# Seven block products for the gates of branches two and three and the recurrence's inputs, in a hybrid diffusion step

## The chip, the cores and the metric

The kernel runs on one core of one Trainium2 chip. The metric is the device time of one execution in microseconds, the median of several runs. A core has TensorE (PE, matrix products into PSUM), VectorE (DVE), ScalarE (ACT) and GpSimd (POOL); SyncE (SP) issues the transfers. Each engine runs its own instructions in a fixed order and waits for the others by semaphores.

## The reference, cut to what matters

One step of a two-layer backbone on 128 context tokens and 512 latent tokens, all float32, width 1024. Each layer:

```python
h = rms_norm(x, norm1_g) * (1 + scale1) + shift1
z = h @ w_in
u_pool, q, k, v, u_lru, u_gate, gates = jnp.split(z, splits, axis=-1)
pool_o = pool_mixer(u_pool, w_pool, pool_scale)                 # branch one
attn_o = neighbourhood_attention(...)                           # branch two (context tokens: full attention)
h_seq, h_final = rg_lru(conv_centred(u_lru, conv_w, conv_b), ...)   # a linear recurrence both ways
lru_o = h_seq * jax.nn.gelu(u_gate)                             # branch three
g = jax.nn.sigmoid(gates.reshape(B, L, 3, D_MODEL))
merged = (g[:, :, 0] * (pool_o @ w_branch[0]) + g[:, :, 1] * (attn_o @ w_branch[1])
          + g[:, :, 2] * (lru_o @ w_branch[2]))
x = x + gate1 * (merged @ w_out)
h2 = rms_norm(x, norm2_g) * (1 + scale2) + shift2
x = x + gate2 * (jnp.square(jax.nn.relu(h2 @ w_up)) @ w_down)
```

`shift1` to `gate2` come from a product of the conditioning vector with `w_mod` (1024 x 6144). `w_in` has 6144 columns: 512 each for u_pool, q, k, v, u_lru and u_gate, then 3 x 1024 for the gates.

## The kernel before

All 640 tokens stand on the free axis, in two halves of 320; channels stand on the partitions. A float32 product is made of three matmuls in a reduced format: each operand is split into a high and a low part, and high x high, high x low and low x high are added up in PSUM. Weights are split when they arrive (ScalarE copies the high part, L227, VectorE subtracts for the low part, L228), activations when they are made.

The work is a list of items. An item is one block of weights with the code that uses it: `k8` is 1024 rows x 128 columns (8 blocks of 128 rows, `product`, L256 to L258), `k4` is 512 rows x 256 columns, `modv` is a block of `w_mod` that VectorE alone multiplies and adds up (`mod_acc`, L517 and L519), and `st` is a pair, 1024 rows x 256 columns, as seven block products. The loop at the end goes through the items: transfers are issued up to three items ahead into three raw tiles of 512 KB (a pair takes two), weights are split one item ahead, then the item's body runs. `mod_next` puts the next `modv` item into the list.

A pair (`st_begin`, `st_product`, `st_body`) is a Winograd form of Strassen's scheme: the weights are seen as 2 x 2 blocks (512 rows x 128 columns), the activations as 2 x 2 blocks (512 channels x 320 tokens). POOL makes four sums of weight blocks (S1 to S4, L272 to L275), the seven blocks a11, S1, S2, a12, S3, S4, a22 are split one after another (L288, L289), each is multiplied with one of the seven activation blocks b11, T1, T2, b21, T3, b22, T4 (12 matmuls each, L295 to L297), and the results are added up: in PSUM where the order allows, else copied out by ScalarE (`keep`, L309) and added by VectorE (`total`, L313). T1 to T4 are made by `sums` from the four blocks of h. Before, only the MLP's first matrix is used in this way, from block 1 on; `sums` runs at the head of the MLP.

Side work stands in Python generators in two queues, `side_a` (attention, norms) and `side_b` (pool mixing, the recurrence `lru`, `sums`). `tick()` after each product runs one step of each, `drain` runs a queue to its end, `defer` puts a piece behind so many ticks. The framework orders the instructions of an engine by this order of tracing and by when their operands are ready in its own model.

A layer, in order: 16 items of w_in for v, k, q and the pool with attention as side work; the gates of branch one (8 `k8` items) with its branch products (4 `k4`); the recurrence's inputs (4 items) and the GELU inputs (4 items) in the order `ORD`; the gates and products of branch two; those of branch three; the output projection; the MLP. The recurrence `lru` runs as side work from its first item to the start of branch three's products. The MLP's head is four `k8` items at once (`head`): their low halves, then the norm of the second half of the tokens (`norm_second`), the rest of the first half with its evictions (L1190 to L1193), and the second half. Then two plain items, two `down` items and the first pair.

Large tiles come from one pool `act` of 13 tiles of 10 KB a partition: x, h, v, q/k, branch operands, T1 to T4. The attention's masks `um` and its probabilities `P` have tiles of their own. `xs_d` is a copy of x in device memory; x is read back for the output projection.

## Time and profile before

| | us |
|---|---|
| median of 3 runs | 2134.58 (2133.09 to 2137.39) |
| the profiled execution | 2134.76 |
| its span, first to last instruction | 2133.0 |
| TensorE busy | 2095.2 (98%) |
| VectorE busy | 1487.4 (70%) |
| ScalarE busy | 1009.3 (47%) |
| POOL busy | 524.5 (25%) |

In the first layer the span runs so: branch one from 216 to 329 us (with the attention's end), the recurrence's and GELU's inputs from 329 to some 400, the products of branch two from 412 on, those of branch three from 504.7, the output projection from 579.6, the MLP head from 640 to 705.6, the rest of the MLP to some 1085. The second layer follows in the same order, its MLP head from 1685 to 1752.2, and ends at 2133. A busy share counts an instruction from its start to its end; matmuls overlap, so the share of TensorE says only that it hardly pauses. Weight loads (PEld) run beside the matmuls.

### The profile page before, as it was taken

The numbers are of one execution on the slowest core, as the hardware profiler recorded it, in microseconds if no ns is written. First come the engines' busy times: TensorE is split into PE (matmuls) and PEld (weight loads), VectorE is DVE, ScalarE is ACT, GpSimd is POOL, SyncE is SP. The second block draws the span as 40 slices with busy tenths as digits, with TensorE's granted clock in tenths as the row PEclk, the third lists the DMA queues.
The fourth block names the chain that finished last, engine by engine and source line by source line (L and its number), as shares of the span: only waits on it lengthen the run. The fifth ranks groups of instructions, "written<-read, shape, count | busy, mean of one in ns | idle before, by whom it ended". The sixth has DMA issues, their size and how long they took to land.

```text
span 2133.0 us, 35830 instructions
## 1 busy us (share of the span) xinstructions
PE 2095.2 (98%) x13916; PEld 1985.1 (93%) x13916; DVE 1487.4 (70%) x2925; ACT 1009.3 (47%) x2058; POOL 524.5 (25%) x567
## 2 busy tenths in 40 slices
PE   8999999999999999999999999999999999999999
PEld 3988899999999999999989888999999999999999
DVE  4776865757669877777687685575667786666665
ACT  4765526664345433333366653367623543333332
POOL 2444300333203221111134440013311231121110
PEclk9999999999999999999999999999999999999999
DMA  9322244325541433333331122442345212222222
GB/s 322 109 60 85 64 135 120 87 88 158 158 115 52 120 102 98 99 99 99 119 117 52 55 74 79 144 119 65 90 124 186 76 50 80 81 83 84 81 80 79
DMA packets 248961, 218.16 MB, mean 102 GB/s; under 512 B 11076, under 2 KB 216408, under 8 KB 248792
## 3 DMA queue, kind: packets, MB, share of 16 engines
q1 hardware_dynamic: 248792, 215.88, 33.5%
q8 instruction: 109, 1.79, 0.4%
q14 instruction: 60, 0.49, 0.1%
HBM read 204.76 MB, written 13.12 MB: 102 GB/s over the span
## 4 chain that ended last, share of the span: by engine, by line
PE 80%; DVE 10%; ACT 4%; DMA 3%; issue 1%; POOL 1%; SPq 0%; ACTq 0%; DVEq 0%; POOLq 0%
PE mm L256 19%; PE mm L257 18%; PE mm L258 18%; PE mm L295 4%; PE mm L297 4%; PE mm L296 4%; PE o L772 2%; DVE wlo L228 2%; PE mmz L296 1%; PE mmz L297 1%; PE mmz L295 1%; DVE t L465 1%; DVE macc L519 1%; PE ptt L759 1%; PE mps L1438 1%
## 5 line engine op out<-in xcount | busy, mean ns | idle before, releaser
L256 PE MATMUL mm<-h,whi 128*128 128x320 f32 x1600 | 507.3, 317 | 10.3 <-DVE rl L1190 7.2
L258 PE MATMUL mm<-h,wlo 128*128 128x320 f32 x1600 | 498.1, 311 | 3.1 <-DVE wlo L228 3.0
L257 PE MATMUL mm<-h,whi 128*128 128x320 f32 x1600 | 498.3, 311 | 2.7 <-DVE h L479 2.0
L228 DVE TENSOR_TENSOR wlo<-raw,whi 128x512 fp32r<-128x512 f32 x396 | 287.4, 735 | 112.6 <-ACT whi L227 110.7
L227 ACT ACTIVATE whi<-raw 128x512 fp32r<-128x512 f32 x396 | 243.5, 626 | 231.4 <-PE mm L257 86.3
L256 PEld LDWEIGHTS mm<-h,whi 128*128 128x128 f32 x1600 | 303.5, 190 | 25.6 <-ACT h L478 7.6
L256 PE MATMUL mm<-u,whi 128*128 128x320 f32 x992 | 308.2, 311 | 4.1 <-DVE x L498 3.4
L257 PEld LDWEIGHTS mm<-h,whi 128*128 128x128 f32 x1600 | 303.6, 190 | 5.4 <-DVE h L479 2.9
L258 PEld LDWEIGHTS mm<-h,wlo 128*128 128x128 f32 x1600 | 303.4, 190 | 4.2 <-DVE wlo L228 4.1
L258 PE MATMUL mm<-u,wlo 128*128 128x320 f32 x992 | 306.5, 309 | 0.0
L257 PE MATMUL mm<-u,whi 128*128 128x320 f32 x992 | 306.5, 309 | 0.0
L498 DVE SCALAR_TENSOR_TENSOR x<-mm,mod,x 128x320 f32<-128x320 f32 (+2 forms) x432 | 175.3, 433 | 116.7 <-PE mm L258 116.3
L519 DVE SCALAR_TENSOR_TENSOR macc<-raw,silc,macc 128x512 f32<-128x512 f32 x280 | 217.5, 799 | 36.8 <-DMA raw<-in_w_mod_dram 35.1
L256 PEld LDWEIGHTS mm<-u,whi 128*128 128x128 f32 x992 | 186.2, 188 | 8.6 <-issue 3.9
L257 PEld LDWEIGHTS mm<-u,whi 128*128 128x128 f32 x992 | 186.3, 188 | 0.1
L258 PEld LDWEIGHTS mm<-u,wlo 128*128 128x128 f32 x992 | 186.2, 188 | 0.0
L272 POOL TENSOR_TENSOR S<-raw 128x512 f32<-128x512 f32 x26 | 34.3, 1320 | 531.8 <-DMA raw<-in_w_up_dram 319.6
L288 ACT ACTIVATE whi<-S 128x512 fp32r<-128x512 f32 x104 | 65.8, 633 | 198.6 <-PE mm L257 144.0
L288 ACT ACTIVATE whi<-raw 128x512 fp32r<-128x512 f32 x78 | 49.4, 633 | 127.1 <-PE mm L257 106.6
L289 DVE TENSOR_TENSOR wlo<-S,whi 128x512 fp32r<-128x512 f32 x104 | 73.0, 703 | 44.4 <-ACT whi L288 44.1
L297 PE MATMUL mm<-T,wlo 128*128 128x320 f32 x312 | 96.5, 309 | 0.5 <-DVE wlo L289 0.5
L295 PE MATMUL mm<-T,whi 128*128 128x320 f32 x312 | 96.4, 309 | 0.0
(303 smaller groups left out, 4657.6 us busy)
## 6 DMA issues: line engine op xcount, KB each, us to landing
raw<-in_w_in_dram SPq DMA_DIRECT2D x96, 512.0 KB, 4.1
raw<-in_w_mod_dram SPq DMA_DIRECT2D x80, 512.0 KB, 3.8
raw<-in_w_up_dram SPq DMA_DIRECT2D x64, 512.0 KB, 3.8
raw<-in_w_down_dram SPq DMA_DIRECT2D x64, 512.0 KB, 3.5
raw<-in_w_branch_dram SPq DMA_DIRECT2D x24, 512.0 KB, 3.5
wm<-in_w_mod_dram SPq DMA_DIRECT2D x8, 1024.0 KB, 12.2
raw<-in_w_out_dram SPq DMA_DIRECT2D x16, 512.0 KB, 4.6
xs_d<-x SPq DMA_DIRECT2D x4, 1280.0 KB, 7.8
```

The lines of the kernel that those rows point to most:

```text
L227: A.activation(hi, rs, AF.Copy)
L228: V.tensor_tensor(lo, rs, f32(hi), op=OP.subtract)
L256: T.matmul(ps, wh, xh, start=(k == 0), stop=False)
L257: T.matmul(ps, wh, xl, start=False, stop=False)
L258: T.matmul(ps, wl, xh, start=False, stop=(k == nk - 1))
L288: A.activation(hi, a, AF.Copy)
L289: V.tensor_tensor(lo, a, f32(hi), op=OP.subtract)
L295: T.matmul(ps, hi[:, k, :], x[:, 0, k, :], start=start and k == 0, stop=False, skip_group_check=True)
L296: T.matmul(ps, hi[:, k, :], x[:, 1, k, :], start=False, stop=False, skip_group_check=True)
L297: T.matmul(ps, lo[:, k, :], x[:, 0, k, :], start=False, stop=k == 3, skip_group_check=True)
L498: V.scalar_tensor_tensor(xa, ps[:, a:b], mod[l][:, gate + m, j:j + 1], xa, op0=OP.mult, op1=OP.add)
L519: V.scalar_tensor_tensor(acc[j], w, silc[:, k, j:j + 1], acc[j], op0=OP.mult, op1=OP.add)
```

## The change

Four pairs per layer take the place of the eight plain items for the recurrence and GELU inputs, and eight pairs that of the sixteen gate items of branches two and three (`z_pair`). For this `sums` now also runs in branch one, from gate 4 on, and again at the MLP head for the new h. A pair needs less room: S1, S2 and S4 follow one another in one tile, S3 overwrites a21, and each sum is made when the split before it has read its place. The tile Z of a pair comes from the PSUM pool that the attention's output has. `tick` inside a pair steps the side queues after every other product only.

`um` and `P` move into one tile `room` of the pool `act`, which gets 14 tiles; it is given back at gate 4, where the attention is driven to its end. The order of inputs is now recurrence 0 and 1, GELU 0 and 1, GELU 2 and 3, recurrence 2 and 3. Modulation items: 4 stand among the inputs where 6 stood, 8 in branch three where 12 stood; four move to the plain items and first `down` items of the MLP, and three further places are added there.

The norm of the second half becomes four pieces of two channel blocks, one at once and one after each of the next three evictions; `sums` is queued after them. The first output product does the first six blocks of both halves, then the last two.

The diff, without the moved code, comments, the changed lines of the loops that call it, and the removed functions that the new ones replace:

```diff
-    act = pool("act", 13)
+    act = pool("act", 14)
...
-    s_p = pool("s", 3)
...
-    um = [cst.tile([128, n], F32, name=f"um{i}") for i, n in enumerate((640, 384, 384))]
...
-        s1, s2, s3, s4 = (t_p.tile([128, 4, 128], F32, tag="t", name=f"S{i}") for i in range(1, 5))
-        G.tensor_tensor(s1, a21, a22, op=OP.add)
-        G.tensor_tensor(s2, s1, a11, op=OP.subtract)
-        G.tensor_tensor(s3, a11, a21, op=OP.subtract)
-        G.tensor_tensor(s4, a12, s2, op=OP.subtract)
-        it["todo"] = deque([a11, s1, s2, a12, s3, s4, a22])
+        s = t_p.tile([128, 4, 128], F32, tag="t", name="S")
+        sub = lambda o, a, b: lambda: G.tensor_tensor(o, a, b, op=OP.subtract)
+        G.tensor_tensor(s, a21, a22, op=OP.add)
+        G.tensor_tensor(a21, a11, a21, op=OP.subtract)
+        it["todo"] = deque([(a11, None), (s, sub(s, s, a11)), (s, sub(s, a12, s)), (a12, None), (a21, None), (s, None),
+                            (a22, None)])
...
-        a = it["todo"].popleft()
+        a, then = it["todo"].popleft()
...
+        if then:
+            then()
...
-        Z = s_ps.tile([128, HALF], F32, tag="s", name="mmz")
+        Z = o_ps.tile([128, HALF], F32, tag="o", name="mmz")
...
-                ahead()
-            tick()
+                nx = it["i"] + 2
+                while nx < len(items) and items[nx - 1]["kind"] == "modv":
+                    nx += 1
+                splits(nx)
...
-    def head(its, done, evict, second=None):
+    def head(its, done, evict, second=None, third=None):
...
+        drain(side_a)
+        if third:
+            third()
...
-        norm_stats(1)
-        norm_apply(l, which, 1)
+
+        def steps():
+            norm_stats(1)
+            for m in range(0, 8, 2):
+                norm_apply(l, which, 1, m, m + 2)
+                yield
+        side_a.append(("norm", steps()))
+        step(side_a)
...
-                P = s_p.tile([128, 384], F32, tag="s", name="P")
+                P = L["P"][0]
+                L["P"].rotate(-1)
...
+    def z_pair(l, L, ci, handlers, pre=None, last=False):
+        def body(it):
+            if "T" not in L:
+                drain(side_b)
+            st_body(it, L["T"], lambda m, half, t: handlers[m](half, t))
+            if last:
+                del L["T"]
+        add("st", w_in[l][:, ci * 128:ci * 128 + 256], body, pre)
...
+                drain(side_a)
...
+            room = unit("room", [128, 2560], F32)
+            L["um"] = [room[:, a:b] for a, b in ((0, 640), (640, 1024), (1024, 1408))]
+            L["P"] = deque(room[:, 1408 + 384 * i:1792 + 384 * i] for i in range(3))
+            for t, a in zip(L["um"], (256, 192, 64)):
+                G.memset(t[:, a:a + 128], 0.0)
...
-        def pre_b(b):
-            def fn():
-                flush()
-                if b == 0:
-                    drain(side_b, ("pool", 3))
-                    L["bo", 0] = L["pool"]
-                    L["merged"] = [unit(f"mg{i}", [128, 4, 640], F32) for i in range(2)]
-                elif b == 1:
-                    drain(side_a)
-                    L["bo", 1] = split_act(L, L.pop("attn"), "ah")
-                    L.pop("v")
-                else:
-                    drain(side_b)
-                    L["bo", 2] = split_act(L, L.pop("lru"), "lh")
-                    L["mh"] = [[unit(f"mh{a}{b}", [128, 2, 4, HALF]) for b in range(2)] for a in range(2)]
-            return fn
-
-        for b in range(3):
-            if b == 1:
-                need_lru = lambda: L.__setitem__("lru", unit("lru", [128, 4, 640], F32))
-                for n, i in enumerate(ORD):
-                    if 0 < n < 7:
-                        mod_next()
-                    if i < 4:
-                        z_item(l, L, COL_GELU + i, gelu_handler(l, L, i))
-                    else:
-                        z_item(l, L, COL_LRU + i - 4, lru_handler(l, L, i - 4), need_lru if i == 4 else None)
-            for m in range(0, 8, 2):
-                for e in range(3):
-                    if e < 2:
-                        z_item(l, L, COL_GATE + 8 * b + m + e, gate_handler(L, b, m + e))
-                    else:
-                        branch_item(l, L, b, m, pre_b(b) if m == 0 else None)
-                    if b != 1:
-                        mod_next()
...
-            while "h free" not in L:
+            while ("free", which) not in L:
...
+        def pre_branch(b, m):
+            def fn():
+                flush()
+                if (b, m) == (0, 0):
+                    drain(side_b, ("pool", 3))
+                    L["bo", 0] = L.pop("pool")
+                    L["merged"] = [unit(f"mg{i}", [128, 4, 640], F32) for i in range(2)]
+                elif (b, m) == (2, 0):
+                    L.pop(("bo", 1))
+                    drain(side_b)
+                    L["bo", 2] = split_act(L, L.pop("lru"), "lh")
+                    L["mh"] = [[unit(f"mh{a}0", [128, 2, 4, HALF])] for a in range(2)]
+                else:
+                    L["merged"][0] = None
+                    for a in range(2):
+                        L["mh"][a].append(unit(f"mh{a}1", [128, 2, 4, HALF]))
+            return fn if (b, m) in ((0, 0), (2, 0), (2, 4)) else None
+
+        def pre_sums():
+            drain(side_a)
+            for k in ("v", "um", "P"):
+                L.pop(k)
+            side_b.append(("sums", sums(0)))
+
+        def pre_lru():
+            flush()
+            L.pop(("bo", 0))
+            L["bo", 1] = split_act(L, L.pop("attn"), "ah")
+            L["lru"] = unit("lru", [128, 4, 640], F32)
+
+        def last_gate(it):
+            L["free", 0] = True
+
+        for b in range(3):
+            if b == 1:
+                for n, (col, fn) in enumerate(((COL_LRU, lru_handler), (COL_GELU, gelu_handler), (COL_GELU + 2, gelu_handler),
+                                               (COL_LRU + 2, lru_handler))):
+                    ct = 2 * (n > 1)
+                    z_pair(l, L, col, [fn(l, L, ct + e) for e in range(2)], pre_lru if n == 0 else None)
+                    mod_next()
+            for m in range(0, 8, 2):
+                if b == 0:
+                    for e in range(2):
+                        z_item(l, L, COL_GATE + m + e, gate_handler(L, b, m + e), pre_sums if m + e == 4 else None,
+                               last_gate if m + e == 7 else None)
+                        mod_next()
+                else:
+                    z_pair(l, L, COL_GATE + 8 * b + m, [gate_handler(L, b, m + e) for e in range(2)], last=(b, m) == (2, 6))
+                    if b == 2:
+                        mod_next()
+                branch_item(l, L, b, m, pre_branch(b, m))
+                if b != 1:
+                    mod_next()
+
+        def out_part(it, m, half, ps=None):
+            x_update(l, 16, m, half, product(it, 0, half, L["mh"], 8, range(6, 8) if ps else None, ps))
...
+        def out_body(m):
+            def body(it):
+                ps = [product(it, 0, half, L["mh"], 8, range(6)) if m == 0 else None for half in range(2)]
+                for half in range(2):
+                    out_part(it, m, half, ps[half])
+            return body
...
-            if (b, e) in ((2, 0), (3, 0)):
+            if (b, e) in ((2, 0), (3, 0), (4, 0)):
                 mod_next()
...
-                if m % 4 == 0:
+                if m % 4 == 0 or (b, m) == (0, 2):
...
-        def second():
-            norm_second(l, 1)
-            side_b.append(("sums", sums()))
-
         add_group("k8", [up_src(i) for i in range(4)],
-                  lambda its, done: head(its, done, lambda *a: evict_up(0, *a), second), pre_up)
+                  lambda its, done: head(its, done, lambda *a: evict_up(0, *a), lambda: norm_second(l, 1),
+                                         lambda: side_b.append(("sums", sums(1)))), pre_up)
         for i in range(2):
             add("k8", up_src(4 + i), plain_body(1, i))
+            mod_next()
```

## Rows read from the trace of the kernel before

**Rows 1.** The page: busy time, share of the span and instructions of each engine.
```profile
PE 2095.2 (98%) x13916; PEld 1985.1 (93%) x13916; DVE 1487.4 (70%) x2925; ACT 1009.3 (47%) x2058; POOL 524.5 (25%) x567
```

**Rows 2.** Stretches: length; PE, PEld, DVE, ACT, POOL busy (instructions); PEclk; DMA share, GB/s.
```profile
216.00:329.00 113.00, 112.62 (x762) 102.06 (x763) 78.08 (x211) 41.16 (x97) 18.71 (x25) 1.00 0.36 107
329.20:412.00 82.80, 81.29 (x546) 78.45 (x545) 51.72 (x74) 54.72 (x90) 11.61 (x18) 1.00 0.36 104
412.00:504.70 92.70, 92.70 (x630) 91.67 (x629) 62.46 (x85) 63.06 (x97) 39.46 (x36) 1.00 0.31 93
504.70:579.60 74.90, 74.89 (x503) 71.78 (x502) 51.25 (x88) 22.23 (x46) 14.64 (x14) 1.00 0.58 171
1699.80:1752.20 52.40, 45.68 (x292) 45.02 (x291) 48.69 (x73) 25.52 (x52) 22.55 (x13) 0.93 0.17 51
1752.00:2081.00 329.00, 329.00 (x2246) 328.94 (x2245) 214.78 (x426) 124.44 (x241) 61.96 (x48) 1.00 0.26 79
```

**Rows 3.** TensorE's waits over the span: us in all, times, longest.
```profile
PE mm L256 <- DVE rl L1190: 7.9, 3, 3.6
PE mm L258 <- DVE wlo L228: 3.0, 2, 1.5
PE mm L256 <- ACT mh L1030: 1.4, 2, 0.8
```

**Rows 4.** Groups by line and form, whole span: busy, mean ns, idle before and its releaser.
```profile
L288 ACT ACTIVATE whi<-S 128x512 fp32r<-128x512 f32 x104 | 65.8, 633 | 198.6 <-PE mm L257 144.0 <-PE mm L296 28.2 <-issue 20.8
L289 DVE TENSOR_TENSOR wlo<-S,whi 128x512 fp32r<-128x512 f32 x104 | 73.0, 703 | 44.4 <-ACT whi L288 44.1
L289 DVE TENSOR_TENSOR wlo<-raw,whi 128x512 fp32r<-128x512 f32 x78 | 68.6, 880 | 39.3 <-ACT whi L288 39.3
L309 ACT ACTIVATE rl<-mm 128x320 f32<-128x320 f32 x52 | 21.9, 421 | 0.0
L313 DVE TENSOR_TENSOR rl<-mm,rl 128x320 f32<-128x320 f32 x52 | 25.6, 492 | 17.3 <-PE mm L297 13.4
L272 POOL TENSOR_TENSOR S<-raw 128x512 f32<-128x512 f32 x26 | 34.3, 1320 | 531.8 <-DMA raw<-in_w_up_dram 319.6 <-DVE u L1207 149.5 <-DVE x L498 62.8
```

**Rows 5.** Groups by line, VectorE, 329.2 to 412 us.
```profile
L519 DVE SCALAR_TENSOR_TENSOR macc<-raw,silc,macc 128x512 f32<-128x512 f32 x20 | 15.7, 798 | 1.0 <-DMA raw<-in_w_mod_dram 0.8
L228 DVE TENSOR_TENSOR wlo<-raw,whi 128x512 fp32r<-128x512 f32 x21 | 14.2, 687 | 17.1 <-ACT whi L227 17.1
```

**Rows 6.** ScalarE, 329.2 to 412 us by line, and its timeline at 351 us.
```profile
L227 ACT ACTIVATE whi<-raw 128x512 fp32r<-128x512 f32 x20 | 12.1, 628 | 12.1 <-DMA raw<-in_w_in_dram 10.6 <-PE mm L257 1.5
L919 ACT ACT_TABLE_LOAD x4 | 5.1, 1283 | 0.1
...
351.34 1.28 ACT L974 ACT_TABLE_LOAD   x1
352.63 0.93 ACT L974 ACTIVATE lt<-lt,nsp 128x644 f32<-128x644 f32 x1
```

**Rows 7.** One line's instructions, 225 to 340 us: duration min/median/max, first and last start.
```profile
L772 PE MATMUL o<-pt,v x78: 272/273/324, 225.9 to 281.4; 128*64 128x128 f32 x78
```

**Rows 8.** Instructions on the tile f of the sums, whole span.
```profile
L1246 DVE TENSOR_TENSOR f<-h x4: 807/810/814, 660.9 to 1718.9; 128x640 f32<-128x640 f32 x4
L1255 POOL TENSOR_TENSOR f<-f,f x4: 1692/2294/2904, 664.9 to 1723.3; 128x640 f32<-128x640 f32 x4
```

**Rows 9.** TensorE's timeline at the second layer's MLP head: start, us, idle before and releaser.
```profile
1703.73 0.61 PE L256 MATMUL mm<-h,whi 128*128 128x320 f32 x1 [3.60 <-DVE rl L1190]
```

**Rows 10.** VectorE's timeline at the same place.
```profile
1697.63 3.81 DVE L465 SCALAR_TENSOR_TENSOR t<-x,amp,rstd 128x192 f32<-128x192 f32 x4
1701.37 1.82 DVE L479 TENSOR_TENSOR h<-t,h 128x320 fp32r<-128x320 f32 x1
```

**Rows 11.** The page: DMA issues of one source: count, KB each, us to landing.
```profile
raw<-in_w_in_dram SPq DMA_DIRECT2D x96, 512.0 KB, 4.1
```

**Rows 12.** One line's instructions, whole span.
```profile
L1237 DVE TENSOR_TENSOR T<-f,T x16: 810/822/2197, 665.5 to 1741.1; 128x640 fp32r<-128x640 f32 x16
```

More of the change, by code (lines that the diff above doesn't have):

```diff
@@ L1220, in plain_body, with sums @@
[L1220 to L1229 removed]
+        def sums(which):
             (b11, b21), (b12, b22) = ((h[0], h[1]) for h in state["h"])
@@ L1322, in build_layer, with plain_body, body @@
+        def plain_body(b, i):
+            def body(it):
+                for half in range(2):
+                    evict_up(b, i, half, product(it, 0, half, state["h"], 8))
+                    tick()
+                if i == 1:
+                    L["free", 1] = True
+            return body
         up_pair = lambda b, e: w_up[l][:, b * 512 + e * 256:b * 512 + e * 256 + 256]
@@ L1476, in start @@
             prev[i.engine] = i
-        for t, a in zip(um, (256, 192, 64)):
-            G.memset(t[:, a:a + 128], 0.0)
         G.memset(bd, 0.0)
```

155 lines of the change are left out of this document (69 added, 86 removed).

## The prediction

> **What bounds the kernel now.** I read the busy shares of the engines first [rows 1], then the table of stretches [rows 2], then TensorE's own waits [rows 3]. The reader is to see that TensorE is busy for 98% of the span and that its waits inside the layers are a few microseconds each. A matmul of 320 columns shows 309 ns in its row, but matmuls overlap: in the long MLP stretch 2246 of them fill 329.00 us, 146.5 ns each, and TensorE never pauses [rows 2]. That pace is my price of a matmul. Time goes, then, where matmuls go, as long as the other engines keep up. Rows 2 also show where they hardly do: VectorE and ScalarE are busy for 51.72 and 54.72 of 82.80 us while the recurrence's inputs are made, for 62.46 and 63.06 of 92.70 us through the gates of branch two, and VectorE for 48.69 of 52.40 us at the second layer's MLP head.
>
> **Matmuls removed.** Two plain items of w_in are 2 x 2 halves x 8 blocks x 3 = 96 matmuls; a pair as seven block products is 7 x 4 x 3 = 84. Each layer has 4 pairs for the recurrence and 8 for the gates of branches two and three, 24 pairs in all: 24 x 12 x 0.1465 = 42.2 us less, 7.0 for each group of four pairs.
>
> **What a pair adds.** Seven weight splits stand in place of four, and three partial products are copied out of PSUM and added back. VectorE: 3 x 0.703 + 4 x 0.880 + 3 x 0.49 = 7.1 us where four splits at 0.687 were 2.7 [rows 4, 5], so 4.4 more. ScalarE: 3 x 0.633 + 3 x 0.421 = 3.2 more. POOL: four sums of 1.32 or a little more, 5.4 more [rows 4]. What hides it is TensorE's own 12.3 us per pair (84 x 0.1465); the rows do not show a pair beside the recurrence, so I take each stretch in turn. Transfers: a pair loads two tiles of 512 KB, as two plain items did, so SP's queue carries the same bytes. The one new wait on POOL is S2's and S4's for the split before them; behind it stand the recurrence's products on POOL, for which VectorE's scans wait, and that is part of the losses below.
>
> *The recurrence's inputs.* TensorE: 4 x 12.3 = 49.2 us, some 4.6 for the block-diagonal products and sums between them, 53.8. VectorE now: 51.72 less 14.2 for splits and 17.3 for six modulation items (15.7, and four first terms that I estimate at half as long, [rows 5]; 2.9 an item) is 20.2 of recurrence work, of which I estimate 2.5 to slip into the next stretch; then four pairs at 7.1 = 28.4 and four modulation items = 11.5: 57.6, a little less because neighbouring rows overlap. ScalarE by the same way: 54.7 - 12.1 + 28 x 0.633 + 12 x 0.421 less some 10 that slips on (estimated from the same stretch's 54.7) = 55 [rows 4, 6]. So all three engines stand at about 54 to 57 us, and TensorE can no longer run ahead: within a pair one PSUM tile is read out and added to again, with one product of 1.76 us in between. I take 4 us lost in each layer: near the 3.8 by which VectorE exceeds TensorE. Bounds are 0 (the overlap hides it) and 9 (the 3.8, and one POOL sum of 1.32 on the path for each of the four pairs).
>
> *Gates of branch two.* VectorE 62.46 + 4 x 4.4 = 80, ScalarE 63.06 + 4 x 3.2 = 76, of 92.7 - 7.0 = 85.7: 93% and 88%. I take 2 us lost per layer, bounds 0 and 5.
>
> *Gates of branch three.* VectorE 51.25 + 17.6 - 11.5 (four modulation items go to other places) = 57 of 67.9. That is 84%, between the MLP stretch's 65%, where seven-product items cost TensorE nothing, and the 93% above [rows 2]. Its modulation items can wait, so I take 0, with 2 per layer as the bound.
>
> *Branch one.* The sums of h that the products need are now also made here, behind gate 4. The waiting attention is driven to its end first; its last product starts at 281.4 us [rows 7], and by the count of matmuls up to there (20 plain items and 72 of the 96 of two branch items) that is ahead of gate 4, so this costs nothing. The sums are 18 VectorE instructions of 0.81, 14.6 us on top of 78.08 of 113 [rows 2, 8], under cover of TensorE; POOL gets eight counterparts of some 2 us. Without that cover I estimate 2 per layer, what one POOL sum on the path costs; I take 0.5.
>
> *Tiles.* The mask tiles and P now share one large tile of a pool of 14 where 13 stood; the memsets move from the start to each layer's begin. These are small POOL instructions ahead of any use: 0. The first out product takes its last two blocks later, but for the second half they stand at the same place in the order as before, and that is where TensorE waits (1.4 for ScalarE's half, as much for VectorE's, [rows 3]): 0, bound -2.8. The wait of 3.0 for a late weight split [rows 3] was among the plain items of the recurrence, which are gone: -3.0, bound 0.
>
> *The MLP head.* Now: TensorE ends the first half, waits 3.6 us for VectorE to empty a PSUM tile, and starts again with a matmul of twice the length [rows 9]; the granted clock over the stretch is 0.93 of its upper level, 2.4 GHz, the slow part being at 1.2 [rows 2]: 0.07 x 52.4 = 3.7 us of clock, of which I estimate 0.8 to lie in the wait itself. The eviction sits behind the whole norm of the second half, and POOL's first sums run beside it: four VectorE instructions take 3.81 and one 1.82 us [rows 10], where a like subtraction takes 0.49 [rows 4]. In pieces, with the sums put behind the norm, the eviction comes in time: 3.6 and 2.9 are to be had in each layer, 13 in all. But VectorE is full here, and four modulation items of 2.9 (four new in the second layer, three in the first, which had one) land in the same stretch: 7 x 2.9 = 20, less 2 x 3.7 for the POOL overlap that goes (3.81 to some 1.5, 1.82 to 0.49) = 13 more on an engine at 93%. What was late because of the norm is next late because of these sums: the evictions of the first down items queue behind them on VectorE, and TensorE waits for those. I take 0, bounds -13 and +13.
>
> **The sum.** The profiled execution took 2134.76 us, its span 2133.0 and 1.8 around it, 0.2 above the runs' median of 2134.58. 2134.8 - 42.2 + 2 x 4 + 2 x 2 + 2 x 0.5 - 3.0 + 0 = 2102.6; I say 2102.
>
> **A rule weighed against a row.** A table load on ScalarE takes 1.28 us and the next activation starts 0.01 us after its end [rows 6]. The Trainium skill, page "ScalarE: Activation LUTs", section "What ACT_TABLE_LOAD costs", puts a switch at about 2.66 us, a drain included. By that the recurrence's stretch, with four loads for the GELU inputs alone and as many again by my reading of its code, would grow on ScalarE by 8 x 1.38 = 11 us in a layer, and the sum to 2125; by the row all of it is in the 54.7 already. The trace disagrees with the page, and I keep the row.
>
> **Rivals.**
> *Everything hides, and the head's gap closes.* For it: the stretches of [rows 2] that hold VectorE at 55 to 69% show next to no TensorE pause, and ScalarE's order is not tied to the source's. Against: the three stretches above. Time: 2134.8 - 42.2 - 3 - 13 + 3 = 2080.
> *The next pair's weights come late.* Four times a layer one pair follows another directly, with three raw tiles of which a pair takes two. The second tile is free when the last of seven splits is done; then 4.1 us to land [rows 11], 1.32 on POOL, 0.63, 0.70: 6.8 us. If that split runs as soon as its buffer is free (after the third product), five products or 8.8 us cover it. If it waits for the fifth product's eviction it is 1.3 + 0.9 later with three products left, 5.3 us: 3.7 late, eight times, 30, of which 8 are in my sum: 2124. For the first: the splits' idle time in [rows 4] ends with TensorE, so they run as buffers come free. Against: ScalarE is full there.
> *POOL holds VectorE up, and the kernel is slower.* Place: the 16 pairs in the recurrence's stretch and branch two. A split of raw weights that runs beside POOL's sums has a mean of 880 ns, one of the sums themselves 703 [rows 4]; a subtraction into T goes from 810 to 2197 [rows 12]. If each of a pair's four sums stopped VectorE once for its length, a pair would cost 5.4 - 0.8 = 4.6 more. It decides from 32.8 / 16 = 2.05 us per pair; at 3 us the time is 2150. Against: the median there is 822. The Trainium skill states the mechanism, page "SBUF — State Buffer", section "Who interferes with whom": a VectorE instruction with both inputs in SBUF and a GpSimd one that reads SBUF exclude each other, the later one blocking outright. The stretched rows, 2197 against 810, agree with it.
>
> **How the numbers follow.** My forecast 0.62, with its own range 2086 to 2115 (the losses of 13 halved and 10 off the head, or the losses doubled); all hidden 0.14; late weights 0.12; POOL 0.08; and 0.04 that late weights and POOL together just cancel the gain. A change under 0.2% (4.3 us) can hardly be told from none here: faster 0.62 + 0.14 + 0.12 = 0.88, same 0.04, slower 0.08. The range leaves out the slower cases and half of the two ends: 2082 to 2126.
>
> **What would show it.** Right: 13628 matmuls of the span's 13916 (288 fewer), at 146 to 148 ns in branch three; the recurrence's stretch at 56 to 60 us with VectorE and ScalarE above 90%; no wait of TensorE for the eviction at the MLP head, but waits for the evictions of the first down items, VectorE there above 95%. Wrong: waits of TensorE for the second weight split after each pair, released by POOL or by a DMA; raw splits far above 0.88 us; the head's gap gone and the stretch shorter than 47 us, which would mean that the modulation items run behind the path.

## The result, and the profile after

The change makes the kernel slower: 2254.63 us (median of 4 runs, 2254.08 to 2254.82) against 2134.68 before, a ratio of 1.0551 with a 95% interval of 1.0532 to 1.0571. I had forecast 2102, in a range of 2082 to 2126.

The page of the changed kernel, busy time of each engine, answers to [rows 1]:

```profile
PE 2105.3 (93%) x13628; PEld 1975.9 (88%) x13628; DVE 1652.1 (73%) x3105; ACT 1086.6 (48%) x2216; POOL 698.0 (31%) x682
```

The 288 matmuls are gone as forecast, yet TensorE now stands still for 7% of the span. No other engine is full. Its longest groups of waits, over the span (us in all, times, longest), answer to [rows 3]:

```profile
PE mm L294 <- ACT rl L308: 35.8, 16, 5.8
PE mm L296 <- DVE wlo L286: 27.0, 12, 3.9
PE mcol L518 <- ACT macc L538: 12.0, 6, 4.6
PE mm L255 <- DVE wlo L225: 8.2, 4, 2.8
PE ptt L772 <- DVE rs L717: 6.8, 1, 6.8
PE ptt L772 <- ACT pt L774: 6.3, 2, 6.0
```

L308 copies a pair's first products out of PSUM, L286 makes the low half of a split weight, L538 copies a modulation row, L717 and L774 belong to the attention. From the starts of all matmuls in both traces: gaps of 0.32 us or more exceed the pace of 0.1465 by 212.0 us in all, 81.6 before; gaps of 0.2 to 0.32 by 82.3 against 52.2. Of these 30 us more, 27 lie where the granted clock is at its lower level, 1.2 GHz (33.6 against 7.1). So 130 us of new waits, 30 of slower matmuls, less 42 of matmuls saved: 118 of the 120 us.

By stage, cut at the starts of the same products in both traces (layer one / layer two). A branch's stretch runs from its first branch product on; its last branch product stands in the stretch of the next first gates:

| stretch | before | after | both layers | my forecast |
|---|---|---|---|---|
| z items, first two gates | 193.6 / 195.7 | 201.8 / 203.7 | +16.2 | 0 |
| rest of branch one | 82.6 / 82.5 | 83.8 / 82.5 | +1.2 | +1 |
| inputs, first gates of branch two | 89.8 / 89.9 | 102.5 / 101.5 | +24.3 | -11.6 |
| branch two, its other gates | 70.5 / 70.5 | 82.3 / 82.3 | +23.6 | -7.5 |
| first gates of branch three | 22.2 / 22.2 | 27.3 / 27.7 | +10.6 | -3.5 |
| branch three, its other gates | 74.9 / 74.9 | 88.8 / 91.9 | +30.9 | -10.5 |
| output projection | 60.4 / 60.6 | 60.4 / 60.4 | -0.2 | 0 |
| MLP head | 65.7 / 67.7 | 65.6 / 65.5 | -2.3 | 0 with the next row |
| rest of the MLP | 382.6 / 329.2 | 390.4 / 336.8 | +15.4 | |

The same stretches as windows of the changed kernel, layer one (columns as in [rows 2]):

```profile
46.10:247.90 201.80, 193.97 (x1273) 170.56 (x1272) 145.87 (x347) 123.29 (x311) 96.96 (x135) 0.98 0.32 93
331.70:434.20 102.50, 86.54 (x522) 80.45 (x521) 80.41 (x102) 64.63 (x116) 43.58 (x43) 0.93 0.26 83
434.20:516.60 82.40, 69.37 (x447) 67.56 (x446) 60.02 (x76) 56.44 (x94) 46.30 (x39) 0.96 0.20 61
543.90:632.70 88.80, 74.92 (x458) 71.73 (x457) 68.69 (x100) 34.33 (x69) 34.72 (x27) 0.90 0.47 145
```

Branch three is the plainest case: VectorE busy 77%, ScalarE 39%, GpSimd 39%, and still TensorE stands. Its second cycle as GpSimd's timeline (start, us, idle before and releaser):

```profile
572.56 0.88 POOL L1043 TENSOR_TENSOR g<-g,mg 128x320 f32<-128x320 f32 x1 [12.16 <-DVE g L1039]
574.07 1.73 POOL L270 TENSOR_TENSOR S<-raw 128x512 f32<-128x512 f32 x1 [0.63 <-ACT mh L1045]
575.88 1.43 POOL L271 TENSOR_TENSOR raw<-raw 128x512 f32<-128x512 f32 x1
577.28 1.33 POOL L1043 TENSOR_TENSOR g<-g,mg 128x320 f32<-128x320 f32 x1
578.57 1.29 POOL L269 TENSOR_TENSOR S<-S,raw 128x512 f32<-128x512 f32 x1
579.82 1.12 POOL L1043 TENSOR_TENSOR g<-g,mg 128x320 f32<-128x320 f32 x1
581.57 1.53 POOL L269 TENSOR_TENSOR S<-raw,S 128x512 f32<-128x512 f32 x1 [0.63 <-DVE wlo L286]
583.06 1.30 POOL L1043 TENSOR_TENSOR g<-g,mg 128x320 f32<-128x320 f32 x1
```

and what stands behind it, on ScalarE and then TensorE:

```profile
578.64 0.47 ACT L1045 ACTIVATE mh<-g 128x320 fp32r<-128x320 f32 x1 [2.16 <-POOL g L1043]
...
584.39 0.47 ACT L1045 ACTIVATE mh<-g 128x320 fp32r<-128x320 f32 x1 [2.42 <-POOL g L1043]
584.77 0.42 ACT L308 ACTIVATE rl<-mm 128x320 f32<-128x320 f32 x1
```
```profile
585.24 0.64 PE L294 MATMUL mm<-T,whi 128*128 128x320 f32 x1 [3.50 <-ACT rl L308]
```

Read it from below. TensorE waits 3.50 us for the copy of the first product. That copy ran at once when ScalarE came to it, but ScalarE works in order and stood behind the copy of a merged result, which waited for GpSimd's add; and GpSimd worked for nearly 12 us on the last cycle's four adds and the next pair's four weight sums, mixed. The matmul behind the wait takes 0.64 us, not 0.31: the granted clock is at 1.2 GHz from 584.1 us, within the wait, to 590.9.

### The profile page after: what moved, and what is told of

Read it like the earlier page. It is cut to its first block, busy times and chain, and to the rows that moved or that the text cites. A ratio compares the mean times of both kernels' runs of the same rounds, so it can differ in the third digit from the quotient of the medians.

```text
span 2253.0 us, 35797 instructions
## 1 busy us (share of the span) xinstructions
PE 2105.3 (93%) x13628; PEld 1975.9 (88%) x13628; DVE 1652.1 (73%) x3105; ACT 1086.6 (48%) x2216; POOL 698.0 (31%) x682
## 4 chain that ended last, share of the span: by engine, by line
PE 62%; DVE 17%; POOL 7%; ACT 5%; issue 4%; DMA 4%; SPq 0%; POOLq 0%; DVEq 0%; ACTq 0%
PE mm L253 12%; PE mm L254 12%; PE mm L255 12%; PE mm L294 5%; PE mm L296 5%; PE mm L295 5%; DVE macc L531 2%; DVE wlo L286 2%; DMA raw<-in_w_in_dram 2%; DMA raw<-in_w_mod_dram 2%; PE mmz L295 2%; PE mmz L294 2%; PE mmz L296 2%; DVE wlo L225 1%; PE o L785 1%
## 5 line engine op out<-in xcount | busy, mean ns | idle before, releaser
L224 ACT ACTIVATE whi<-raw 128x512 fp32r<-128x512 f32 x300 | 187.0, 629 | 180.8 <-PE mm L295 70.3
L253 PE MATMUL mm<-h,whi 128*128 128x320 f32 x832 | 267.5, 323 | 6.2 <-ACT wu L224 2.7
L270 POOL TENSOR_TENSOR S<-raw 128x512 f32<-128x512 f32 x50 | 68.0, 1360 | 652.2 <-DMA raw<-in_w_up_dram 371.1
L254 PE MATMUL mm<-h,whi 128*128 128x320 f32 x832 | 261.2, 315 | 7.1 <-DVE h L484 5.1
L255 PE MATMUL mm<-h,wlo 128*128 128x320 f32 x832 | 259.6, 313 | 0.0
L225 DVE TENSOR_TENSOR wlo<-raw,whi 128x512 fp32r<-128x512 f32 x300 | 210.9, 708 | 48.0 <-ACT whi L224 45.8
L294 PE MATMUL mm<-T,whi 128*128 128x320 f32 x600 | 195.0, 325 | 40.0 <-ACT rl L308 35.8
L286 DVE TENSOR_TENSOR wlo<-raw,whi 128x512 fp32r<-128x512 f32 x200 | 172.4, 869 | 61.6 <-ACT whi L285 61.4
L285 ACT ACTIVATE whi<-raw 128x512 fp32r<-128x512 f32 x200 | 125.0, 629 | 187.3 <-PE mm L254 101.0
L296 PE MATMUL mm<-T,wlo 128*128 128x320 f32 x600 | 194.0, 323 | 20.8 <-DVE wlo L286 20.8
L285 ACT ACTIVATE whi<-S 128x512 fp32r<-128x512 f32 x150 | 94.6, 631 | 238.1 <-PE mm L254 137.7
L295 PE MATMUL mm<-T,whi 128*128 128x320 f32 x600 | 192.1, 320 | 0.0
L286 DVE TENSOR_TENSOR wlo<-S,whi 128x512 fp32r<-128x512 f32 x150 | 128.3, 856 | 67.1 <-ACT whi L285 67.0
L253 PEld LDWEIGHTS mm<-h,whi 128*128 128x128 f32 x832 | 158.5, 191 | 17.2 <-issue 7.1
## 6 DMA issues: line engine op xcount, KB each, us to landing
wm<-in_w_mod_dram SPq DMA_DIRECT2D x8, 1024.0 KB, 12.3
```

What stands on the lines that cost most here:

```text
L224: A.activation(hi, rs, AF.Copy)
L225: V.tensor_tensor(lo, rs, f32(hi), op=OP.subtract)
L253: T.matmul(ps, wh, xh, start=(k == 0), stop=False)
L254: T.matmul(ps, wh, xl, start=False, stop=False)
L255: T.matmul(ps, wl, xh, start=False, stop=(k == nk - 1))
L285: A.activation(hi, a, AF.Copy)
```

## The experiments

Each is the changed kernel with the edit shown, unless another base is named. The runs of before stand beside each set.

**E1 to E4: which part loses where.** E1, E2 and E3 put back plain products:

```diff
# E1: all gates and inputs plain, no operand sums in the mixer
-                z_pair(l, L, col, ...)                  # inputs
-                z_pair(l, L, COL_GATE + 8 * b + m, ...) # gates
+                z_item(l, L, ...)                       # as before
# E2: z_pair only for b == 2; the operand sums during branch two
# E3: z_pair for b == 1 and 2; the inputs plain, the operand sums from the fifth gate on
# E4: the first step of the operand sums under behind(PE)
-            side_b.append(("sums", sums(0)))
+            side_b.append(("sums", late(sums(0))))     # late: with behind(PE): next(steps)
```

> All of the mixer's gates and inputs as plain products again; the tiles in the room, the one weight-sum tile, the norm in pieces and the MLP half stay as in the changed kernel. Stage by stage the changed kernel is 8.2 us (up to the second gate), 2.5 (rest of branch one), 11.4 (inputs of recurrence and GELU), 16.8 (branch two), 14 (branch three) and 7.7 (MLP behind its head) longer per layer than before. Theory A (the pairs and their operand sums make the loss where they stand): only the MLP's 2 x 7.7 us is left, 2134.7 + 15 = 2150 us. Rival B (the room's tiles hold up the attention in the z stage): the z stage's 2 x 8.2 us stays too, 2166 us.

> Pairs only for the gates of branch three; inputs and gates of branch two plain; the operand sums run during branch two's gates. Theory A (each stage's own pairs cost what that stage lost): branch three's 2 x 14 us stays, so 2150 + 28 = 2178 us, and branch two loses little. Rival C (the pairs lose because the recurrence's work, left over from branch two, is late): with plain inputs and gates before it the recurrence is done in time and branch three's pairs gain their forecast 5.3 us a layer, 2150 - 11 = 2139 us.

> Pairs for the gates of branches two and three, inputs of recurrence and GELU plain; the operand sums run during the inputs. Theory A: branch two's 2 x 16.8 us on top of E2, 2178 + 34 = 2212 us. Rival C: the late inputs cause most of branch two's loss, so well under 2180 us.

> The changed kernel with the operand sums of the mixer tied behind TensorE's product of the fifth gate. Theory A (the order puts the sums into the attention, where VectorE waits 5.4 us for GpSimd's part of a sum with a softmax behind it): the z stage is 193.6 us again, 2254.6 - 2 x 8 = 2239 us. Rival B (the attention is late because of the room or because it is drained at the fifth gate): the z stage stays at 202 us and the time at 2254 us or above.

Measured: E1 2140.93 (1.0021, 1.0010 to 1.0033), E2 2207.85 (1.0333, 1.0307 to 1.0359), E3 2227.79 (1.0421), E4 2253.73 (1.0546).

E1 is 9 us below theory A's 2150 and far from rival B: the z stage is 193.6 us again. So the pairs and their sums make nearly all of the loss, and the room's tiles none.

E2 is 30 us above theory A. With the sums beside it, branch two takes 84.8 us a layer for 70.5, although its gates are plain; branch three with its first gates loses 18.5, although the inputs and gates ahead of it are plain. Of these, 11 to 12 stand behind branch three's first product, where no instruction of the recurrence is left. So rival C, late work of the recurrence, does not explain branch three.

E3 is 16 us above theory A, and against rival C too: behind plain inputs branch two's other gates still take 82.5 and 82.9 us, as in the changed kernel. Its z stage, where the sums stand as in the changed kernel, is as long as there (202.8 and 205.8).

E4 tells nothing of the order. Its tie queues only TensorE's instructions, of which the sums have none, and VectorE's order stayed as it was; E9 repeats it.

**E5 to E8: what holds branch three.** Four edits, each of one suspect:

```diff
# E5
-            G.tensor_tensor(mg, mg, g, op=OP.add)      # and: G.tensor_tensor(g, g, mg, ...)
+            V.tensor_tensor(mg, mg, g, op=OP.add)      # and: V.tensor_tensor(g, g, mg, ...)
# E6
-            A.activation(kept[n], ps, AF.Copy)
+            V.tensor_copy(kept[n], ps)
# E7: no mod_next() in branch three, its eight items dropped
# E8: st_begin, for pairs of w_in
-        G.tensor_tensor(s, a21, a22, op=OP.add)        # and the three subtractions
+        V.tensor_tensor(s, a21, a22, op=OP.add)
```

> The changed kernel with the merge adds of branches two and three (g and mg of the branch handler) on VectorE in place of GpSimd. Branch three from its first gates takes 116.1 and 119.6 us in the two layers of the changed kernel and 97.1 before. Theory D (GpSimd's queue: in a cycle of branch three it works off four weight sums and four merge adds, some 12 us in one piece, and ScalarE's copy of the first product out of PSUM stands behind the copies that wait for those adds): the stretch falls below 105 us, the whole by 25 us or more, to 2230 us. Rival E (VectorE is too full for the pairs): four more additions of 0.5 us a cycle on VectorE, the stretch stays at 116 us or grows, the whole 2255 us or above.

> The changed kernel with the copies of the first three products out of PSUM on VectorE in place of ScalarE, in every pair. Theory F (ScalarE's queue alone holds TensorE's next product in the shared PSUM tile): the waits for rl L308, 35.8 us in 16, go, and with the half clock behind them the time falls by 35 us or more, to 2220 us. Theory D (the splits of the weights are as late as the copies, since they wait for GpSimd's sums): the waits move to the second halves of the weights, and the time stays within 10 us of 2255. Rival E: three more 0.4 us copies on VectorE a pair make it longer than 2265 us.

> The changed kernel without the eight modulation items of branch three in each layer (those 8 columns of the modulation stay zero: their loads, VectorE's products and their sums are left out). Theory G (the pair's two raw tiles land late, since the modulation holds the third one, so every sum and split starts late): the pairs' loads go out earlier, branch three falls from 116 and 120 us to under 105, and the whole to 2235 us or less. Rival E (VectorE too full) says the same of the time, but the raw tiles would still land as late. Theory D: GpSimd's eight operations a cycle remain, so branch three stays above 110 us.

> The changed kernel with the four weight sums of each mixer pair on VectorE in place of GpSimd. Theory D (GpSimd's queue): as with the merge adds moved, the stretch of branch three falls below 105 us, and the waits for the second weight halves in the inputs and branch two (13.3 us a layer) shrink, whole 2225 us or less. Rival E (VectorE too full): VectorE gets about 4 x 0.7 us a pair more, branch two grows, whole 2255 us or above.

| | time, ratio (interval) | inputs and branch two | branch three |
|---|---|---|---|
| changed kernel | 2254.63, 1.0551 (1.0532 to 1.0571) | 184.8 / 183.8 | 116.1 / 119.6 |
| E5 | 2219.96, 1.0382 (1.0364 to 1.0401) | 181.5 / 178.5 | 102.1 / 103.8 |
| E6 | 2266.02, 1.0597 (1.0570 to 1.0623) | 185.0 / 186.9 | 114.7 / 118.9 |
| E7 | 2229.84, 1.0424 (1.0405 to 1.0443) | 183.1 / 183.9 | 105.5 / 106.7 |
| E8 | 2204.94, 1.0313 (1.0292 to 1.0334) | 170.2 / 169.4 | 101.6 / 103.3 |
| before | 2134.68 | 160.3 / 160.4 | 97.1 / 97.1 |

E5 and E8 give VectorE more to do and the kernel gets 35 and 50 us faster, as theory D said: against rival E (VectorE too full). Branch three's other gates in E5 and E8, layer one, columns as above:

```profile
539.20:614.80 75.60, 70.08 (x458) 65.66 (x456) 69.86 (x114) 32.47 (x68) 19.16 (x12) 1.00 0.53 165
527.40:603.00 75.60, 69.78 (x456) 65.74 (x456) 68.10 (x109) 33.60 (x68) 16.41 (x14) 1.00 0.54 164
```

VectorE is busy there for as long as in the changed kernel (69.86 and 68.10 us against 68.69), and the stretch is 13 us shorter. So VectorE's total is not what made 88.8 us of it.

E6 moves the copy away from the stuck queue, and nothing is won: the waits move to VectorE's copies and ScalarE's splits. Its largest waits:

```profile
PE mm L294 <- DVE rl L308: 42.7, 18, 7.0
PE mm L294 <- ACT whi L285: 18.8, 5, 6.3
```

Theory F falls: ScalarE's queue hands the delay on and doesn't make it. At 2266 us E6 doesn't part D from E, whose bounds I had put at 2265.

E7 gains 25 us, which D did not foresee (it said above 110 us); theory G, late raw tiles, had the time (2235 or less) and nearly the stretch (under 105). The traces of the first layer's three pairs behind branch three's first product show how early a pair's second weight tile is asked for, counted to the pair's first matmul, and how long the pair then takes from its first matmul to its last:

| | asked for ahead, us | the pair, us |
|---|---|---|
| changed kernel | 9.1, 8.0, 9.1 | 17.9, 20.0, 20.1 |
| E5 | 8.5, 7.7, 8.3 | 15.1, 14.6, 15.0 |
| E7 | 14.8, 12.6, 12.6 | 13.8, 16.9, 16.4 |
| E8 | 8.9, 5.6, 8.5 | 15.0, 15.6, 13.9 |

In E5 and E8 the tiles are asked for no earlier than in the changed kernel, and the pairs are shorter by 3 to 6 us; in E7 they are asked for 3.5 to 6 us earlier, and two of the three pairs are longer than E5's. So late tiles alone are not the cause. The modulation has a share in branch three's loss; whether by its raw tiles or by some 23 us of VectorE's work a layer (eight items at the 2.9 of the forecast), E7 doesn't say.

VectorE's groups by line and form tell a second thing. Changed kernel, then E8 (where the lines are one lower):

```profile
L286 DVE TENSOR_TENSOR wlo<-S,whi 128x512 fp32r<-128x512 f32 x150 | 128.3, 856 | 67.1 <-ACT whi L285 67.0
L1046 DVE SCALAR_TENSOR_TENSOR mh<-g,mh 128x320 fp32r<-128x320 f32 x32 | 23.9, 746 | 21.2 <-ACT mh L1045 21.2
```
```profile
L287 DVE TENSOR_TENSOR wlo<-S,whi 128x512 fp32r<-128x512 f32 x150 | 121.1, 807 | 55.3 <-ACT whi L286 55.2
L1047 DVE SCALAR_TENSOR_TENSOR mh<-g,mh 128x320 fp32r<-128x320 f32 x32 | 18.3, 576 | 9.5 <-ACT mh L1046 9.5
L271 DVE TENSOR_TENSOR S<-raw 128x512 f32<-128x512 f32 x24 | 16.5, 689 | 8.4 <-DMA raw<-in_w_in_dram 8.2
L270 DVE TENSOR_TENSOR S<-S,raw 128x512 f32<-128x512 f32 x24 | 16.4, 685 | 0.0
```

The four kinds of sums that moved are 17.0 + 16.5 + 16.4 + 16.4 = 66.3 us in E8 (two of the four are shown), yet VectorE's busy time grows from 1652.1 to 1660.1 only: its other instructions became 58 us shorter in sum as GpSimd's sums left from beside them.

**E9 to E11: the order of the sums, the ticks, and all together.** `tied` queues the first step of the operand sums behind the last instruction of each of the three engines that make them:

```diff
# E9
-            side_b.append(("sums", sums(0)))
+            side_b.append(("sums", tied(sums(0))))
+        def tied(steps):
+            with behind(DVE, ACT, mybir.EngineType.Pool):
+                next(steps)
+            yield
+            yield from steps
# E10
-MD2 = 2
+MD2 = 4
# E11: E5 + E8 + E9 + E10
```

> E4 again with a tie that holds: the first step of the mixer's operand sums is queued on VectorE, ScalarE and GpSimd behind what stood last on each of them when the fifth gate began, so behind the last softmax (in E4 the tie concerned TensorE alone, and VectorE's order was that of the changed kernel). Theory A (order): the z stage falls from 201.8 and 203.7 to 194 and 196 us, the whole to 2239 us, if the sums then still end before the first pair. Rival H (the sums come late instead, and the first pair's operands or GpSimd's queue give the time back): the z stage falls, and branch one or the inputs grow by as much, the whole stays above 2248 us.

> The changed kernel with the modulation's transposes (mcol) issued four ticks behind ScalarE's copy instead of two. A pair ticks seven times in 12.3 us where two plain gates tick four times in 14.1 us. Theory I (two ticks inside a pair are too short for ScalarE's copy, and TensorE, in order, stands behind it): the waits for macc L538, 12.0 us in 6, and the half clock behind them go, the whole falls by 10 to 20 us. Rival (ScalarE's copy is late by whole items): the wait only moves, the whole stays within 4 us of 2255.

> The edits of E5, E8, E9 and E10 together: merge adds and the mixer pairs' weight sums on VectorE, operand sums behind the last softmax, mcol later. If the causes are separate (GpSimd's queue, the order at the fifth gate, the ticks), the gains add up: from E8's 2205 us less 16 (z stage), 10 (mcol) and some 10 (merge adds), 2169 us. If VectorE is full by then, it stays above 2195 us. Below 2135 us the seven-product forms would pay.

The place of E9 in the changed kernel, VectorE's timeline, then ScalarE's and TensorE's:

```profile
227.37 0.83 DVE L1161 TENSOR_TENSOR f<-h 128x640 f32<-128x640 f32 x1
233.57 0.82 DVE L1166 TENSOR_TENSOR f<-f,h 128x640 f32<-128x640 f32 x1 [5.37 <-POOL f L1163]
234.31 0.55 DVE L708 CUSTOM_DVE_ANT_0 room<-s,room 128x384 f32<-128x384 f32 x1
```
```profile
234.90 0.61 ACT L709 ACTIVATE room<-room,mn 128x384 f32<-128x384 f32 x1 [11.97 <-DVE mn L708]
```
```profile
238.00 0.90 PE L772 MATMUL ptt<-cs,room 128*128 128x128 f32 x3 [6.02 <-ACT pt L774]
```

A sum's step stands ahead of the softmax L708 in VectorE's order and waits for GpSimd; ScalarE idles 11.97 us, TensorE 6.02. With the tie the z stage is 195.5 and 197.4 us, 6.3 less in each layer. Most of it comes back in the inputs, 107.1 and 107.6 for 102.5 and 101.5, with new waits of TensorE of 2.5 us each for an eviction on VectorE (mg) and on ScalarE (g). The whole: 2247.50 (1.0521, 1.0505 to 1.0536). So both parts are true: the order causes most of the z stage's loss, and rival H, for which I had asked 2248 or more, has most of the account.

E10: 2257.30 (1.0564). Theory I falls: the waits for macc are 16.8 us in 4 where they were 12.0 in 6. In the changed kernel ScalarE stands without work for 5.24 us, behind an operand sum of VectorE, and comes to that copy 5 us later:

```profile
339.64 0.74 ACT L1151 ACTIVATE T<-f 128x640 fp32r<-128x640 f32 x1 [5.24 <-DVE f L1184]
...
345.01 0.57 ACT L538 ACTIVATE macc<-mps 64x512 f32<-64x512 f32 x1
```

E11: 2180.32 (1.0208, 1.0188 to 1.0229), 15 us below my figure for a full VectorE and 11 above the 2169 for separate causes; the gains as measured one by one (34.7, 49.7, 7.1 and -2.7) would make 2165.8. Branch three with its first gates takes 96.6 and 96.2 us, inputs and branch two 168.8 and 169.4.

By the cuts of the stage table, E11's profile is 45 us longer than that of before, both layers together: 17.7 in the rest of the MLP, 12.1 in the rest of branch one, 8.3 in the inputs, 9.1 in branch two, 4.3 in the first gates of branch three; branch three's other gates are 5.6 shorter (72.1 and 72.1 for 74.9). In branch one (88.7 and 88.5 us for 82.6 and 82.5) TensorE stands in each layer at the last branch product, and ScalarE's split ahead of it waits for the weights to land:

```profile
328.67 0.64 PE L253 MATMUL mm<-po,whi 128*128 128x320 f32 x1 [4.24 <-ACT whi L224]
```
```profile
327.99 1.15 ACT L224 ACTIVATE whi<-raw 128x512 fp32r<-128x512 f32 x2 [6.60 <-DMA raw<-in_w_branch_dram]
```

**E12 to E14: what is left.** E12 and E14 start from E11, E13 from E1:

```diff
# E12
-                side_b.append((("lru", ct), lru(l, L, ct)))
+                L.pop(("lu", ct))
# E13
             add("k8", up_src(4 + i), plain_body(1, i))
-            mod_next()
-            if (b, e) in ((2, 0), (3, 0), (4, 0)):
+            if (b, e) in ((2, 0), (3, 0)):
-                if m % 4 == 0 or (b, m) == (0, 2):
+                if m % 4 == 0:
# E14: st_begin, pairs of branch three
-        s = t_p.tile([128, 4, 128], F32, tag="t", name="S")
+        s1, s2, s3, s4 = (t_p.tile(...) for i in range(1, 5))  # as before, all four at once
```

> E11 with the recurrence left out (convolution, gates, scans and their product; its branch then multiplies the GELU's output alone), pairs and everything else kept. In E11 the inputs up to the first product of branch two take 94 us and branch two 75, where the forecast's terms make 89.8 - 12.3 + 4 = 81.5 and 70.5 - 5.3 + 2 = 67. Theory J (the recurrence's work on VectorE and ScalarE is what the pairs' splits and copies stand behind): both fall to the forecast's lengths within 2 us, less what the recurrence's own products took. Rival K (the pair's own chain, split, sum in the one tile, split, is too long by itself): branch two stays above 72 us.

> E1 (no pairs in the mixer) with the modulation items of the MLP back in the slots of the kernel before, none behind the two plain products that follow the head. What is left of the change is the room for the attention's tiles, the single weight-sum tile and the norm in pieces. Theory L (the modulation's work on VectorE behind the head is what makes E1 6 us longer): 2135 us, no difference from before. Rival M (the single weight-sum tile lengthens the first pair): 2140 us as E1. If the head gains as well, 2131 us.

> E11 with four separate tiles for the weight sums of branch three's pairs, all four sums made when the pair's splits begin, on VectorE. Branch three from its first gates takes 96.6 us in E11, 97.1 before, and by the forecast's term 97.1 - 7 = 90. Rival K (the chain through the one sum tile): 93 us or less. Theory J or a chain that starts late for want of raw tiles: 96 us, no change.

E12: 2114.28 (0.9894, 0.9880 to 0.9907). Its windows of branch two and of the first gates of branch three:

```profile
415.20:473.30 58.10, 58.10 (x399) 58.10 (x397) 40.41 (x72) 25.18 (x48) 0.00 (x0) 1.00 0.25 77
473.30:492.80 19.50, 19.50 (x135) 19.36 (x133) 16.44 (x31) 7.94 (x16) 0.00 (x0) 1.00 0.32 103
```

TensorE doesn't pause once, at the upper clock (2.4 GHz): three cycles of 84 + 48 matmuls at 0.1465 are 58.0. Theory J holds for branch two, and rival K falls: with nothing of the recurrence beside them the pairs gain what I forecast. Of the 66 us between E11 and E12 the recurrence's own 192 matmuls (13628 less 13436) are 28; 38 were in the way. The inputs still take 83.7 and 81.6, where J said 81.5 less the 36 matmuls that went there (5.3): 5 to 8 us are not the recurrence's. Branch three's other gates, where no recurrence runs in either, take 71.8 and 70.1, still 3 to 5 us above the pace of their 456 matmuls. E14: 2181.99 (1.0211), no gain, branch three at 98.5 and 100.5 us, against rival K again. E13: 2137.83 (1.0003, 0.9994 to 1.0012): no difference from before, theory L. E1's excess came from the slots of the modulation; the room, the single sum tile and the norm in pieces together give and cost nothing.

**E15: a version that should win.** From E2, with the operand sums at branch one's fifth gate again and tied, VectorE for branch three's merge adds and its pairs' weight sums, E13's slots, and two more places for modulation items ahead of branch three.

> Pairs for the gates of branch three alone, with what the runs showed: merge adds of branch three and the weight sums of its pairs on VectorE, operand sums begun behind the last softmax at branch one's fifth gate (the last of them when branch two's gates are done), the MLP's modulation in the slots of the kernel before. From E13 (2138 us): if branch three with its first gates takes what E12 showed without the recurrence beside it, 91 us in place of 97, less 2 us for the last operand sum, the gain is 2 x 4 us, 2130 us, faster than both kernels. If the recurrence's end still stands beside the first pair as in E11 (96.6 us) and the sums cost branch one their 6 us again, 2148 us.

2140.66 (1.0018, 1.0008 to 1.0029): not faster than before, and between the two times that I gave. Branch three with its first gates takes 97.5 and 94.0 us where 97.1 stood, not the 91 hoped for, and branch two 72.3 for 70.5: the gain of 3 us in one layer pays for the sums, no more. No version run here that does the whole work beats the kernel before.

## Why the prediction was wrong, point by point

**Matmuls removed: right.** 288 fewer at 0.1465 us; E12 shows the whole gain of a pair in branch two, where nothing else is in the way then.

**The step that failed: "What hides it is TensorE's own 12.3 us per pair".** I priced a pair by engine totals and took what fitted under TensorE's time as hidden, 2 and 4 us lost a layer in branch two and the inputs and 0 in branch three. Measured against the saving, the inputs lost 42 us in both layers (24.3 + 17.6), branch two 34, branch three 55.5 (10.6 + 30.9 + 14). GpSimd's 5.4 us a pair were in no total, only in a bound (one sum of 1.32) and in a rival; in branch three they stand in one queue with four merge adds, in the chain VectorE, GpSimd, ScalarE, TensorE, all in order. E5 and E8 show it: with either half of that work gone from GpSimd, 35 and 50 us come back over the whole kernel, 14 to 16 a layer of them in branch three with its first gates.

The total itself was too small as well. I had 57 us of VectorE in the 67.9 us of branch three (84%), for four pairs where that stretch holds three; it measures 68.69, more than my whole stretch. In E11, where GpSimd has no work there, VectorE does 24 instructions more in 67.10. Such a total costs a few us at most, by an estimate from E11, where the stretch takes 72.1; it does not make the 14 and 17 that the stretch grew. At 88.8 us VectorE is busy 77%, and what TensorE waits for is an order of work.

**"TensorE can no longer run ahead": right in kind.** The wait for the copy out of the shared PSUM tile is the largest one, 35.8 us. I gave it 4 us a layer in the inputs only, where it is 3.3 us in the first layer; 13.1 lie in the first layer's branch three. E6 shows that the copy itself isn't the cause.

**Branch one: the cost was in another stage.** The attention's last product starts ahead of the fifth gate in the trace of before, so I took its end for safe. But the sums were ordered into the attention, ahead of the stage for which I had counted them, and that stage, the z items with the first two gates, lost 8 us a layer; the tie of E9 takes 6.3 of them away there.

**The MLP head: the wait shorter, not by the pieces alone; the sum at its upper bound.** The wait for the eviction is 1.2 us at most where it was 3.6. But the norm in pieces alone doesn't do this: E1 and E13 have the same pieces, and that wait is 3.0 and 3.7 us there. What shortens it in the changed kernel stays open. The head is 2.3 us shorter in both layers, and the rest of the MLP 15.4 longer: +13.1, the upper bound I had given. The place was another than I said. No wait for the evictions of the first `down` items shows; the loss lies in the first 100 matmuls behind the head, where the first pair is, 7.5 and 6.4 us above their pace in the two layers, 0.8 and 0.0 before. It goes with the slots of the modulation: in E1 the first layer's head has four such loads and the excess is 6.9, the second's has none and it is 0.0; in E13, which differs from E1 in the slots alone, it is 0.0 in both.

**The rival of GpSimd** came nearest in sign, with 0.08 and 2150 us. Its place, the inputs and branch two, leaves out branch three, where most was lost. Its mechanism, instructions of VectorE that get longer beside GpSimd's, shows in E8's 58 us; the sign that I had named for it, raw splits far above 0.88 us, doesn't (869 ns), but the splits of sums went from 703 to 856. The Trainium skill, page "SBUF — State Buffer", section "Who interferes with whom", has such a rule: a VectorE instruction with two inputs in SBUF contends with a GpSimd one that reads SBUF. The trace agrees with it: the mean of L1046, two inputs in SBUF, is 746 ns, and 485 in E11 (L1047 there), where GpSimd has nothing to do in that stretch. How much of E5's and E8's gain is the shorter instructions and how much the shorter queue, no run here divides. In branch three VectorE's busy time did not fall; and GpSimd's eight instructions of the cycle shown, each at the shortest of its kind in it (0.88 and 1.29 us), would still take 8.7 of their 11.8 us, by my estimate. So the queue is the larger part there, as far as is known; for the inputs and branch two it stays open.

**The recurrence as a competitor** was in my sums as busy time, 93% of VectorE at most. E12 puts its price in E11's form, beyond its own matmuls, at 38 us. What keeps the inputs 11 to 13 us a layer above the pace of their 484 matmuls even without it (3 us above it before, with it) stays open.

## What to carry to other kernels

In this kernel, fewer matmuls for more work on the other engines paid only where the longest chain through their queues, not their busy share, fitted under the saved form's matmuls. So write down, for each hand-over of a PSUM tile, every instruction that stands ahead of it in each in-order queue and what that one waits for. The same pairs that ran free in the MLP, with two items between them and GpSimd busy for 20% of the time, stood still in branch three with one item between them and GpSimd at 39%. Before a side job is started earlier, look where the order puts its first step on every engine it uses; a tie on one engine holds that engine alone.

## What the runs showed of the hardware that I had not expected

Moving 66.3 us of additions from GpSimd to VectorE raised VectorE's busy time by 8.0 us and took 139 from GpSimd's (698.0 to 558.9). And TensorE's waits were paid for again behind them, with some 27 us of slower matmuls at the lower clock over the span. In branch three the mean granted clock is 0.90 of the upper level, 2.4 GHz, in the changed kernel, and 1.00 in E11 over the window that answers to it:

```profile
522.00:594.10 72.10, 69.47 (x457) 65.71 (x457) 67.10 (x124) 32.54 (x67) 0.00 (x0) 1.00 0.56 172
```
